# More modulation rows on TensorE, another order in the first layer, and padded pools, in a float32r network of two blocks

## The chip, the cores and the metric

One core of a Trainium2 chip runs the whole program. The metric is the device time of one execution in microseconds (us), the median of several. Before the change it is 2746.2 us (three runs, 2743.26 to 2751.51).

## The reference

The program computes two blocks on 512 tokens of width 1024, with 256 context tokens beside them in the first. The first block is two mixer layers with adaptive modulation by a condition vector; the change works mostly in the first of them:

```
m = silu(cond) @ w_mod + b_mod              # shift, scale, gate: 3 x 1024, for x and for the context
h = x * (1 + scale) + shift
z = h @ w_in                                # 1024 -> a, ga, u, v, gb of 512 each
ya = multiscale_pool(a) * silu(ga)          # windows 2, 4, 8, 16, then a 128x128 product per group
vn = (v - mean) * rsqrt(var + 1e-6)         # per token and head of 128
yb = u * (w_s @ vn + b_s) * silu(gb)        # per chunk of 128 tokens and head
x = layer_norm(alpha * x + gate * (concat(ya, yb) @ w_out))
```

The second layer is a Fourier mix beside a latent attention. The second block is twice: a gated feed-forward (1024 to 2816 to 1024), an attention of three kinds, and a second feed-forward.

## The kernel before

Activations lie with features on the 128 partitions and tokens along the free axis. Every product is kept near float32: each operand is split into a rounded float32r part H and the remainder L, and `mm3` issues three matmuls (H by H, H by L, L by H) into one PSUM bank. So the weights are split on the chip: `wload` fetches a 128x1024 block (tag `ws`, two buffers), ScalarE rounds it to `wh` (line 92), and `s.w_eng` subtracts for `wl` (line 93). `wnext` asks for blocks four ahead of the product that uses them, and each block fetched lets `s.rate` jobs of the list `s.jobs` go. The engine of line 93 is GpSimd (POOL) from the start of `ab`, the first layer, into the second; elsewhere it is mostly VectorE (DVE).

In `ab`, `mods(k)` makes two rows of modulation (k and 8 + k). A row in `ON_PE` is eight small float32 matmuls `pm` (line 548) and an addition on DVE (line 549); another is made on DVE by a custom multiply-and-reduce (line 475) for each of the two conditions, then line 552. These read `fbt`, silu of the condition on all partitions, which comes as a 1 MB transfer `crow` and passes ScalarE. `modx(k)` then modulates a block of tokens, and line 485 makes its L part on DVE. Six banks `pv` gather v, with the activations as stationary operand.

After that vn is normalised on DVE: statistics, an rsqrt of small operations (lines 194 to 202), and 24 operations at line 610. The projections `proj` stand in the order u, gb, u of the next head; after three of them come the six small matmuls `pf` (line 637), which need all of vn. DVE adds the bias, multiplies by u and by silu(gb), and splits the result into Y. The jobs in this time are the other modulation rows of this layer and all 24 of the next, two customs or one each, into borrowed buffers `xs` and `ctmp`. Then come the four pool groups (`pa`, `pb`, and `pp`, 128x128 products), and the output projection, which reads Y. A scheduler orders each engine's instructions.

Each tile pool begins where the pools opened before it end. `w` (weights) and `x` (activations and held blocks) begin 192 bytes past a multiple of 2048; the pools opened after the small pool `fc` begin elsewhere: `h` and `mo` (second block) and `fc` itself at 1856, `c`, `cdy`, `cdm`, `cda`, `cdf` at 384, `y` and `mw` and `yt` at 1632.

Of the kernel before, what the change touches and what calls it, by code (L numbers as in the profile page):

```python
# [9 lines left out]
F32 = mybir.dt.float32  # L10
F32R = mybir.dt.float32r
I32 = mybir.dt.int32
AF = mybir.ActivationFunctionType
ALU = mybir.AluOpType
# [3 lines left out]
P = 128  # L18
T = 512
NEG = -1e30  # L20
MAGIC = 0x5F3759DF
ALPHA = 4.0 ** 0.25
ON_PE = (0, 8, 10, 13, 15)
HALF = (slice(0, 256), slice(256, 512))
ALL = slice(0, 512)

# [5 lines left out]
class Net:  # L32
# [415 lines left out]
    def ab_weights(s):  # L448
        I = s.I
        for c in range(4):  # L450
            s.wpush(I["ab_v"][c], 1024)
        for i in (8, 12, 9, 13, 10, 14, 11, 15):
            s.wpush(I["ab_in"][i], 1024)
        s.wpush(I["pool_w"], 512)
        for i in (0, 4, 1, 5, 2, 6, 3, 7):
            s.wpush(I["ab_in"][i], 1024)
        for m in range(8):
            s.wpush(I["ab_out"][m], 1024)
# [55 lines left out]
    def ab(s):  # L514
        nc, tc, I = s.nc, s.tc, s.I
        s.psum(mm=range(6), t=(6, 7))
        s.w_eng = nc.gpsimd
        fbt = s.xp.tile([P, 4096], F32, tag="fb", name="fbt")
        s.first = ExitStack()
        s.fc = s.first.enter_context(tc.tile_pool(name="fc", bufs=1, reuse_waits="tile"))  # L520
# [2 lines left out]
        X = s.new_xh()  # L523
        C = [c_p.tile([P, 8, 256], F32R, tag="c" + t, name="c" + t) for t in "HL"]
        s.mods_start()
        b1 = c_p.tile([P, 16], F32, name="b1")
        nc.vector.tensor_copy(b1[:, 0:8], s.vec("ab_b", 0, 8))
        nc.vector.tensor_scalar(b1[:, 8:16], s.vec("ab_b", 8, 8), 1.0, None, op0=ALU.add)
        xs = s.xp.tile([P, 4096], F32, tag="x", name="xs")
        pv = [s.bank("pv") for _ in range(6)]  # L530

        def tokx(k, t):
            return s.xk(X, k, slice(t * P, t * P + P)) if t < 4 else s.xk(C, k, slice((t - 4) * P, (t - 3) * P))
# [6 lines left out]
        def mods(k):  # L540
            for m in (k, 8 + k):
                d = s.ab_m[:, m]
                if m in ON_PE:
                    w = mbuf()
                    nc.sync.dma_start(w, I["ab_mod"][m])
                    pm = s.bank("pm", "t")
                    for j in range(8):
                        nc.tensor.matmul(pm[:, 0:2], w[:, j * P:(j + 1) * P], s.sc[:, j], start=(j == 0), stop=(j == 7))
                    nc.vector.tensor_scalar(d, pm[:, 0:2], b1[:, m:m + 1], None, op0=ALU.add)
                else:  # L550
                    s.mod_dve(s.ab_m, I["ab_mod"], m, 2, fbt, mbuf)
                    nc.vector.tensor_scalar(d, d, b1[:, m:m + 1], None, op0=ALU.add)

        def modx(k):
            st = xs[:, k % 5 * 768:k % 5 * 768 + 768]
            nc.sync.dma_start(st, I["x"][:, k])
            s.modulate(X, k, ALL, st[:, :T], s.ab_m[:, 8 + k, 0:1], s.ab_m[:, k, 0:1], st[:, :T])
            s.modulate(C, k, slice(0, 256), st[:, T:], s.ab_m[:, 8 + k, 1:2], s.ab_m[:, k, 1:2], st[:, T:])
# [1 line left out]
        mods(0)  # L560

        for v in range(2):
            row = fbt[:, v * 1024:(v + 1) * 1024]
            nc.sync.dma_start(row, I["crow"][:, v * 1024:(v + 1) * 1024])
            nc.scalar.activation(row, row, AF.Silu)
        modx(0)
        mods(1)
        for k in range(8):
            if k % 2 == 0:
                W = s.wnext(1)  # L570
            if k < 7:
                modx(k + 1)
            if k < 6:
                mods(k + 2)
            w = [x[:, k % 2 * T:(k % 2 + 1) * T] for x in W]
            for t in range(6):
                s.mm3(pv[t], tokx(k, t), w, k == 0, k == 7)
        mx.close()
        ctmp = c_p.tile([P, 2048], F32, tag="cx", name="ctmp")
        spare = []  # L580

        def buf():
            spare.append(spare.pop(0))
            return spare[-1]
        spare += [xs[:, 3072:], ctmp[:, :1024], ctmp[:, 1024:]]
        nc.sync.dma_start(s.ident, I["ident"])
        nc.sync.dma_start(fbt[:, 2048:2560], I["sgu_b"])
        nc.sync.dma_start(fbt[:, 2560:3072], I["sgu_w"])
        edge = c_p.tile([P, 4, 16], F32, name="edge")
        nc.sync.dma_start(edge, I["edge"])  # L590
        with tc.tile_pool(name="y", bufs=1, reuse_waits="tile") as yp, tc.tile_pool(name="yt", bufs=1, reuse_waits="tile") as tp:
            Y = [yp.tile([P, 8, 768], F32R, name="y" + t) for t in "HL"]
# [11 lines left out]
            ve = c_p.tile([P, 24], F32, name="ve")  # L604
            nc.vector.tensor_scalar(ve, mv[:, :, 1], 1e-6, None, op0=ALU.add)
            rv = s.rsqrt(ve, 24, "sgu")
            for t in range(6):
                for h in range(4):
                    j = t * 4 + h
                    nc.vector.tensor_scalar(vn[:, t, h], vn[:, t, h], mv[:, j, 0:1], rv[:, j:j + 1], op0=ALU.subtract, op1=ALU.mult)  # L610

            def proj(ahead=4):

                W = s.wnext(ahead)
                a, b = s.bank("pa"), s.bank("pb")
                s.lin(a, W, X, 8, ALL)
                s.lin(b[:, :256], W, C, 8, slice(0, 256))
                return a, b[:, :256]
# [3 lines left out]
            def ysplit(k, src, sl):  # L622
                s.split(Y[0][:, k, sl], Y[1][:, k, sl], src)

            u = proj()
            for g in range(4):
                gb = proj()
                if g < 3:
                    u2 = proj()
                if g == 0:  # L630
                    s.jobs = [(lambda i=i: s.mod_dve(s.ab_m, I["ab_mod"], i, 2, fbt, buf)) for i in range(16, 24)]
                    s.jobs += [(lambda i=i: s.mod_dve(s.cd_m, I["cd_mod"], i, 2 if i < 16 else 1, fbt, buf)) for i in range(24)]
                G = tp.tile([P, 768], F32, tag="G", name="G")
                t_ = tp.tile([P, 768], F32, tag="T", name="T")
                pf = s.bank("pf", "t"), s.bank("pf", "t")
                for c in range(6):
                    nc.tensor.matmul(pf[c // 4][:, c % 4 * P:(c % 4 + 1) * P], vn[:, c, g], fbt[:, 2560 + g * P:2560 + (g + 1) * P], start=True, stop=True)
                for i, sl in enumerate(PARTS):
                    n = sl.stop - sl.start
                    bs = fbt[:, 2048 + g * P:2048 + (g + 1) * P].unsqueeze(1).to_broadcast([P, n // P, P])  # L640
                    tt = t_[:, sl]
                    nc.vector.tensor_tensor(tt.rearrange("p (c i) -> p c i", i=P), pf[i][:, :n].rearrange("p (c i) -> p c i", i=P), bs, op=ALU.add)
                    nc.scalar.activation(G[:, sl], gb[i], AF.Silu)
                    nc.vector.tensor_tensor(tt, tt, u[i], op=ALU.mult)
                    nc.vector.tensor_tensor(tt, tt, G[:, sl], op=ALU.mult)
                    ysplit(4 + g, tt, sl)
                u = u2


            LP = 800  # L650
            A, S1, S2 = ctmp[:, 0:LP], ctmp[:, LP:2 * LP], fbt[:, 3072:3072 + LP]
            spare[:] = [xs[:, j * 1024:(j + 1) * 1024] for j in range(4)]
            nc.gpsimd.memset(ctmp, 0.0)
            nc.gpsimd.memset(S2, 0.0)
            at = (slice(8, 520), slice(536, 792))
# [43 lines left out]
                old = new  # L699
            pool_out(3, *old)  # L700

            while s.jobs:
                s.jobs.pop(0)()
            s.add_bias(s.ab_m, "ab_b", 16, 24)

            nc.vector.tensor_scalar(s.ab_m[:, 16:24], s.ab_m[:, 16:24], 1.0 / ALPHA, None, op0=ALU.mult)
            s.add_bias(s.cd_m, "cd_b", 0, 16)
            s.add_bias(s.cd_m, "cd_b", 16, 24, 1)
            nc.vector.tensor_scalar(s.cd_m[:, 8:16], s.cd_m[:, 8:16], 1.0, None, op0=ALU.add)

            s.gb = s.fc.tile([P, 2, 8, 2], F32, name="gb")
            for v in range(2):
                nc.vector.tensor_tensor(s.gb[:, 0, :, v], s.cd_m[:, 8:16, v], s.vec("ab_g", 0, 8), op=ALU.mult)
                nc.vector.tensor_tensor(s.gb[:, 1, :, v], s.cd_m[:, 8:16, v], s.vec("ab_lb", 0, 8), op=ALU.mult)
                nc.vector.tensor_tensor(s.gb[:, 1, :, v], s.gb[:, 1, :, v], s.cd_m[:, 0:8, v], op=ALU.add)
            ag = c_p.tile([P, 2, 8], F32, name="ag")
            nc.vector.tensor_scalar(ag[:, 0], s.vec("ab_g", 0, 8), ALPHA, None, op0=ALU.mult)
            nc.vector.tensor_scalar(ag[:, 1], s.vec("ab_lb", 0, 8), ALPHA, None, op0=ALU.mult)
# [16 lines left out]
            def fin(m, seg, ps):  # L735
                v, sl = s.SEG[seg]
                s.ln_fin(V[v], m, sl, ps, s.ab_m[:, 16 + m, v:v + 1], acc[seg])

            for m in range(5):
                W = s.wnext()  # L740
                a, b = s.bank("pa"), s.bank("pb")[:, :256]
                omm(a, W, slice(0, T))
                omm(b, W, slice(T, 768))
                fin(m, 0, a[:, 0:256])
                fin(m, 1, a[:, 256:512])
                fin(m, 2, b)
            Ws = s.wlast(3)

            def last(seg, sl):
# [356 lines left out]
    def mix(s, l, st, mktail):  # L1106
# [12 lines left out]
        for k in range(8):  # L1119
            nc.sync.dma_start(s.spill[:, k], s.x[:, k])  # L1120

        ll = s.tp.tile([P, 2], F32, tag="ll", name="ll")
        nc.vector.tensor_tensor(ll, s.vec(f"lq_{l}", 0, 2), s.vec(f"lk_{l}", 0, 2), op=ALU.mult)
        pl = s.bank("pl", "t")
        nc.tensor.matmul(pl[:, 0:2], s.ones, ll, start=True, stop=True)
# [374 lines left out]
def prep_first(inp, A, vec):  # L1500
    i = lambda n: inp[n][0]
    cc = np.stack([i("c"), inp["c_ctx"]])
    vec("c", np.ascontiguousarray(cc.reshape(2, 8, P).transpose(2, 1, 0)).reshape(P, 16))
    A["crow"] = np.ascontiguousarray(np.broadcast_to(cc.reshape(1, 2048), (P, 2048)))
    vec("ab_b", rows(i("ab_b_mod")))
    vec("cd_b", rows(i("cd_b_mod")))
    vec("ab_g", rows(i("ab_ln_g")))
# [128 lines left out]
```

## Time and profile before

| | us |
|---|---|
| median of three runs | 2746.2 |
| lowest, highest | 2743.26, 2751.51 |
| profiled execution | 2743.77 |
| its span, first to last instruction | 2741.7 |
| PE busy in it | 2632.7 |
| DVE, ACT, POOL busy in it | 1504.3, 1056.6, 323.0 |

The profiled execution is 2.4 us below the median and 2.1 us above its own span. PE is TensorE, ACT ScalarE. PEclk is the clock granted to TensorE, as a share of its full level. A timeline row gives the start, the duration, and in brackets the idle time before and what ended it. A matmul's duration covers its passage through the array, so the pace of a run of matmuls is read from start to start; one row in float32 (line 548) counts two passes for each matmul of the code.

### The profile page before, as it was taken

How to read it: one execution, taken by the hardware profiler on the slowest of the kernel's cores; microseconds unless marked ns; L12 is line 12 of the kernel's file. 1: busy time of each engine (PE TensorE's matmuls, PEld its weight loads, DVE VectorE, ACT ScalarE, POOL GpSimd, SP SyncE). 2: the span in 40 equal slices, each digit the busy share in tenths (PEclk: the TensorE clock that was granted, in tenths of full speed). 3: DMA queues.
4: the chain of work that ended last, by engine and by line, in shares of the span. 5: the costliest groups of instructions: out<-in, count | busy, mean ns of one | idle time of the engine just before them, and what ended most of it. 6: DMA issues, size and time to landing. Idle time of an engine off the chain costs nothing. (4 is left out here: it accounts for less than half of the span.)

```text
span 2741.7 us, 36211 instructions
## 1 busy us (share of the span) xinstructions
PE 2632.7 (96%) x13676; PEld 2230.8 (81%) x13676; DVE 1504.3 (55%) x2886; ACT 1056.6 (39%) x1951; POOL 323.0 (12%) x300
## 2 busy tenths in 40 slices
PE   7898999998999999999999999999999998999998
PEld 6787987887888888878888888888888877988887
DVE  7895632888545345675853336633336666642434
ACT  4122533664444233454543224432223454432222
POOL 2323344003000011001200002000001001200000
PEclk9999999998999999999999999999999999999999
DMA  7353123004998247654693323963237655232221
GB/s 271 135 193 120 44 82 101 32 30 166 312 315 291 91 141 234 195 154 140 219 317 109 99 84 108 318 221 100 92 101 243 208 156 156 76 100 99 94 94 60
DMA packets 133966, 418.15 MB, mean 153 GB/s; under 512 B 17376, under 2 KB 20960, under 8 KB 133792
## 3 DMA queue, kind: packets, MB, share of 16 engines
q1 hardware_dynamic: 133792, 415.84, 45.7%
q8 instruction: 108, 1.77, 0.3%
q14 instruction: 66, 0.54, 0.1%
HBM read 314.32 MB, written 73.40 MB: 141 GB/s over the span
## 5 line engine op out<-in xcount | busy, mean ns | idle before, releaser
L92 ACT ACTIVATE wh<-ws 128x1024 fp32r<-128x1024 f32 (+2 forms) x335 | 345.3, 1033 | 865.4 <-PE pd L148 238.6
L93 DVE TENSOR_TENSOR wl<-ws,wh 128x1024 fp32r<-128x1024 f32 (+1 forms) x267 | 318.3, 1192 | 164.4 <-ACT wh L92 161.1
L147 PE MATMUL pg<-xH,wh 128*128 128x512 f32 x672 | 262.2, 390 | 0.0
L149 PE MATMUL pg<-xH,wl 128*128 128x512 f32 x672 | 261.7, 389 | 0.0
L148 PE MATMUL pg<-xL,wh 128*128 128x512 f32 x672 | 261.6, 389 | 0.0
L149 PE MATMUL pd<-hH,wl 128*128 128x512 f32 x632 | 249.6, 395 | 0.0
L147 PE MATMUL pd<-hH,wh 128*128 128x512 f32 x632 | 249.6, 395 | 0.0
L148 PE MATMUL pd<-hL,wh 128*128 128x512 f32 x632 | 249.6, 395 | 0.0
L148 PE MATMUL pu<-xL,wh 128*128 128x512 f32 x640 | 249.2, 389 | 0.0
L147 PE MATMUL pu<-xH,wh 128*128 128x512 f32 x640 | 249.1, 389 | 0.0
L149 PE MATMUL pu<-xH,wl 128*128 128x512 f32 x640 | 249.0, 389 | 0.0
L93 POOL TENSOR_TENSOR wl<-ws,wh 128x1024 fp32r<-128x1024 f32 (+1 forms) x68 | 171.5, 2529 | 326.1 <-ACT wh L92 317.0
L247 POOL TENSOR_TENSOR accf<-accf,sq 128x256 f32<-128x256 f32 x48 | 39.7, 847 | 1390.1 <-ACT sq L246 1390.1
L399 DVE TENSOR_TENSOR ht<-ht,pu 128x512 f32<-128x512 f32 x80 | 54.9, 686 | 182.5 <-PE pu L149 180.4
L149 PEld LDWEIGHTS pg<-xH,wl 128*128 128x128 f32 x672 | 126.1, 188 | 26.1
L148 PEld LDWEIGHTS pg<-xL,wh 128*128 128x128 f32 x672 | 126.2, 188 | 26.0
L147 PEld LDWEIGHTS pg<-xH,wh 128*128 128x128 f32 x672 | 126.2, 188 | 26.1
L148 PEld LDWEIGHTS pd<-hL,wh 128*128 128x128 f32 x632 | 118.6, 188 | 28.8
L149 PEld LDWEIGHTS pd<-hH,wl 128*128 128x128 f32 x632 | 118.6, 188 | 28.8
L147 PEld LDWEIGHTS pd<-hH,wh 128*128 128x128 f32 x632 | 118.6, 188 | 28.7
L147 PEld LDWEIGHTS pu<-xH,wh 128*128 128x128 f32 x640 | 120.1, 188 | 25.0
L148 PEld LDWEIGHTS pu<-xL,wh 128*128 128x128 f32 x640 | 120.1, 188 | 24.9
(622 smaller groups left out, 5982.6 us busy)
## 6 DMA issues: line engine op xcount, KB each, us to landing
ws<-ffn_gate SPq DMA_DIRECT2D x88, 512.0 KB, 3.5
ws<-ffn_up SPq DMA_DIRECT2D x88, 512.0 KB, 3.5
hl<-eh SPq DMA_DIRECT2D x64, 512.0 KB, 6.8
hl<-el SPq DMA_DIRECT2D x64, 512.0 KB, 6.8
ws<-ffn_down SPq DMA_DIRECT2D x64, 512.0 KB, 3.6
wh<-hl SPq DMA_DIRECT2D x58, 512.0 KB, 4.3
wl<-hl SPq DMA_DIRECT2D x58, 512.0 KB, 6.0
es<-wqk SPq DMA_DIRECT2D x32, 512.0 KB, 5.8
```

Of the source, the lines that this page charges most:

```text
L92: nc.scalar.activation(wh[:, :n], st[:, :n], AF.Copy)
L93: s.w_eng.tensor_tensor(wl[:, :n], st[:, :n], f(wh[:, :n]), op=ALU.subtract)
L147: mm(out, A[0], B[0], start=start, stop=False)
L148: mm(out, A[0], B[1], start=False, stop=False)
L149: mm(out, A[1], B[0], start=False, stop=stop)
L247: (eng or nc.gpsimd).tensor_tensor(acc[0], acc[0], sq, op=ALU.add)
L399: nc.vector.tensor_tensor(t, t, pu, op=ALU.mult)
```

## The change

The first layer: three more rows of modulation go to PE (1, 9, 12 and 14 for 13), so the rows of both first blocks are made there. `crow` goes: sixteen float32 matmuls `pr` (line 566) spread silu(c) over the partitions, and ScalarE copies them to `fbt`. Line 93 is on DVE in `ab` as elsewhere. Half of vn's normalisation goes to ScalarE (with nb = -mean * rstd), head by head. Jobs get three buffers of their own, `mj`, and wait for the last DVE instruction of the normalisation; they go at 1.4 per block instead of 2.2. The head loop starts with two u projections, and does `pf`, the bias and the product with u ahead of the gb projection. The rest of the jobs and what reads the second layer's rows move behind five output projections.

The padding: `b1` moves to `fc`, and `gb`, `edge` and `ll` get a longer tile, so that `fc` is 2048 bytes. It begins at 131264 instead of 130880, which is 192 past a multiple of 2048, and so do after it `h`, `mo`, `ma`, `c`, `cdy`, `cdm`, `cda`, `cdf`, `y` and `yt`.

```diff
-ON_PE = (0, 8, 10, 13, 15)
+ON_PE = (0, 1, 8, 9, 10, 12, 14, 15)
-        s.w_eng = nc.gpsimd
+        s.w_eng = nc.vector
+        nc.sync.dma_start(s.ident, I["ident"])
-        b1 = c_p.tile([P, 16], F32, name="b1")
+        b1 = s.fc.tile([P, 16], F32, name="b1")
...
         for v in range(2):
-            row = fbt[:, v * 1024:(v + 1) * 1024]
-            nc.sync.dma_start(row, I["crow"][:, v * 1024:(v + 1) * 1024])
-            nc.scalar.activation(row, row, AF.Silu)
+            for h in range(2):
+                pr = s.bank("pr")
+                for j in range(4):
+                    nc.tensor.matmul(pr[:, j * P:(j + 1) * P], s.sc[:, 4 * h + j, v:v + 1].to_broadcast([P, P]), s.ident, start=True, stop=True)
+                nc.scalar.activation(fbt[:, v * 1024 + h * T:v * 1024 + (h + 1) * T], pr, AF.Copy)
...
+        buf = lambda: c_p.tile([P, 1024], F32, tag="mj", name="mj", bufs=3)
-        edge = c_p.tile([P, 4, 16], F32, name="edge")
+        edge = c_p.tile([P, 256], F32, name="edge")[:, :64].rearrange("p (g t) -> p g t", t=16)
...
-            for t in range(6):
-                for h in range(4):
+            nb = c_p.tile([P, 24], F32, name="nb")
+            nc.vector.scalar_tensor_tensor(nb, mv[:, :, 0], -1.0, rv, op0=ALU.mult, op1=ALU.mult)
+            for h in range(4):
+                for t in range(6):
                     j = t * 4 + h
-                    nc.vector.tensor_scalar(vn[:, t, h], vn[:, t, h], mv[:, j, 0:1], rv[:, j:j + 1], op0=ALU.subtract, op1=ALU.mult)
+                    if t % 2:
+                        nc.scalar.activation(vn[:, t, h], vn[:, t, h], AF.Identity, scale=rv[:, j:j + 1], bias=nb[:, j:j + 1])
+                    else:
+                        normed = nc.vector.tensor_scalar(vn[:, t, h], vn[:, t, h], mv[:, j, 0:1], rv[:, j:j + 1], op0=ALU.subtract, op1=ALU.mult)
...
-            u = proj()
+            us = [proj(), proj()]
+            s.rate = 1.4
             for g in range(4):
-                gb = proj()
-                if g < 3:
-                    u2 = proj()
...
+                    nc.vector.tensor_tensor(tt, tt, us[g][i], op=ALU.mult)
+                gb = proj()
+                if g < 2:
+                    us.append(proj())
...
-            while s.jobs:
+            while len(s.jobs) > 24:
                 s.jobs.pop(0)()
...
+            s.gb = s.fc.tile([P, 384], F32, name="gb")[:, :32].rearrange("p (a m v) -> p a m v", a=2, m=8)
...
-        ll = s.tp.tile([P, 2], F32, tag="ll", name="ll")
+        ll = s.tp.tile([P, 56], F32, tag="ll", name="ll")[:, :2]
```

PE at the start of the program; `pm` is a row of modulation, `pr` the spread condition, `pv` the v projection. Before:

```order
L548 MATMUL pm_175<-sc_156,wm_173 128x2 x8
L548 MATMUL pm_187<-sc_156,wm_185 128x2 x8
L147 MATMUL pv_164<-wh_224,xH_152 128x512
L147 MATMUL pv_165<-wh_224,xH_152 128x512
L148 MATMUL pv_164<-wl_225,xH_152 128x512
L149 MATMUL pv_164<-wh_224,xL_153 128x512
L148 MATMUL pv_165<-wl_225,xH_152 128x512
L149 MATMUL pv_165<-wh_224,xL_153 128x512
```

After:

```order
L566 MATMUL pr_192<-ident_76,sc_156 128x128
L548 MATMUL pm_170<-sc_156,wm_168 128x2 x8
L566 MATMUL pr_192<-ident_76,sc_156 128x128 x3
L548 MATMUL pm_182<-sc_156,wm_180 128x2 x8
L566 MATMUL pr_198<-ident_76,sc_156 128x128 x4
L566 MATMUL pr_204<-ident_76,sc_156 128x128 x4
L566 MATMUL pr_210<-ident_76,sc_156 128x128 x4
L548 MATMUL pm_231<-sc_156,wm_229 128x2 x8
L147 MATMUL pv_253<-wh_225,xH_152 128x512
L147 MATMUL pv_254<-wh_225,xH_152 128x512
L548 MATMUL pm_243<-sc_156,wm_241 128x2 x8
L147 MATMUL pv_255<-wh_225,xH_152 128x512
```

Two rows of modulation stood ahead of the first `pv`; now it is three and the sixteen `pr`, and a fourth row stands after two more matmuls.

DVE at the end of vn's rsqrt; `junk` names the customs of the jobs, `tsgu` and `ysgu` are the rsqrt's, `xs` is vn. Before:

```order
L198 SCALAR_TENSOR_TENSOR tsgu<-tsgu 128x24
L475 ISA junk,ab_m<-ctmp,fbt 128x1024
L475 ISA ab_m 128x1
L199 SCALAR_TENSOR_TENSOR ysgu<-tsgu,ysgu 128x24
L475 ISA junk,ab_m<-xs,fbt 128x1024
L475 ISA ab_m 128x1
L200 TENSOR_TENSOR tsgu<-ysgu 128x24
L475 ISA junk,ab_m<-xs,fbt 128x1024
L475 ISA ab_m 128x1
L201 SCALAR_TENSOR_TENSOR tsgu<-tsgu,ve 128x24
L202 SCALAR_TENSOR_TENSOR ysgu<-tsgu,ysgu 128x24
L610 TENSOR_SCALAR xs<-xs,mv,ysgu 128x128 x24
```

After, from the same place to the end of the normalisation:

```order
L93 TENSOR_TENSOR wl<-ws,wh 128x1024
L194 TENSOR_SCALAR ysgu<-ve 128x24
L196 TENSOR_TENSOR tsgu<-ysgu 128x24
L197 TENSOR_TENSOR tsgu<-tsgu,ve 128x24
L198 SCALAR_TENSOR_TENSOR tsgu<-tsgu 128x24
L199 SCALAR_TENSOR_TENSOR ysgu<-tsgu,ysgu 128x24
L200 TENSOR_TENSOR tsgu<-ysgu 128x24
L201 SCALAR_TENSOR_TENSOR tsgu<-tsgu,ve 128x24
L202 SCALAR_TENSOR_TENSOR ysgu<-tsgu,ysgu 128x24
L606 SCALAR_TENSOR_TENSOR nb<-mv,ysgu 128x24
L613 TENSOR_SCALAR xs<-xs,mv,ysgu 128x128 x12
L475 ISA junk,ab_m<-mj,fbt 128x1024
```

The customs have gone from between the rsqrt's operations, one of line 93 stands ahead of them (another one earlier), and DVE normalises 12 blocks instead of 24.

## Rows read from the trace of the kernel before

**Rows 1.** The page, engines: busy time, share of the span, instructions.
```profile
PE 2632.7 (96%) x13676; PEld 2230.8 (81%) x13676; DVE 1504.3 (55%) x2886; ACT 1056.6 (39%) x1951; POOL 323.0 (12%) x300
```

**Rows 2.** The first layer by windows: length, busy of five engines, PEclk, DMA share, GB/s.
```profile
80.00:100.00 20.00, 15.96 (x73) 12.88 (x72) 19.86 (x42) 3.37 (x5) 9.05 (x3) 0.79 0.42 145
100.00:120.00 20.00, 16.55 (x81) 13.69 (x81) 19.17 (x34) 2.44 (x5) 2.89 (x2) 0.87 0.40 136
200.00:220.00 20.00, 16.89 (x84) 14.26 (x84) 19.93 (x38) 4.08 (x8) 5.66 (x2) 0.91 0.52 179
220.00:240.00 20.00, 11.12 (x57) 9.12 (x56) 15.83 (x22) 7.63 (x16) 5.48 (x2) 0.79 0.56 175
```

**Rows 3.** PE's waits, first 330 us: total us, times, longest.
```profile
PE pp L147 <- ACT yH L236: 11.1, 2, 8.9
...
PE pf L637 <- DVE xs L610: 4.0, 6, 2.7
...
PE pa L147 <- DVE T L644: 3.4, 1, 3.4
```

**Rows 4.** DVE's timeline, 33 to 97 us: start, duration, operation.
```profile
33.05 3.30 DVE L475 CUSTOM_DVE_ANT_0 junk<-wm,fbt 128x1024 bf16<-128x1024 f32 x1
...
36.53 1.22 DVE L475 CUSTOM_DVE_ANT_0 junk<-wm,fbt 128x1024 bf16<-128x1024 f32 x1
...
57.75 0.22 DVE L552 TENSOR_SCALAR ab_m<-ab_m,b 128x2 f32<-128x2 f32 x1
...
66.88 1.68 DVE L603 BATCH_NORM_AGGREGATE mv<-bns 128x2 f32<-128x6 f32 x24
...
73.48 2.37 DVE L196 TENSOR_TENSOR tsgu<-ysgu 128x24 f32<-128x24 f32 x1
...
88.92 8.42 DVE L610 TENSOR_SCALAR xs<-xs,mv,ysgu 128x128 f32<-128x128 f32 x24
```

**Rows 5.** PE's timeline at the start of the kernel.
```profile
5.50 6.96 PE L548 MATMUL pm<-sc,wm 128*128 128x2 f32 x32 [5.50 <-DMA wm<-ab_mod]
16.25 1.22 PE L147 MATMUL pv<-wh,xH 128*128 128x512 f32 x2 [3.79 <-ACT wh L92]
...
23.99 1.84 PE L548 MATMUL pm<-sc,wm 128*128 128x2 f32 x16
```

**Rows 6.** The page, line 93 on its two engines: busy, mean ns, idle before.
```profile
L93 DVE TENSOR_TENSOR wl<-ws,wh 128x1024 fp32r<-128x1024 f32 (+1 forms) x267 | 318.3, 1192 | 164.4 <-ACT wh L92 161.1
...
L93 POOL TENSOR_TENSOR wl<-ws,wh 128x1024 fp32r<-128x1024 f32 (+1 forms) x68 | 171.5, 2529 | 326.1 <-ACT wh L92 317.0
```

**Rows 7.** Windows 64 to 247 and 480 to 620 us, all engines.
```profile
64.00:247.00 183.00, 162.25 (x891) 140.18 (x890) 157.45 (x287) 43.13 (x73) 59.70 (x22) 0.93 0.48 167
...
480.00:620.00 140.00, 136.16 (x865) 115.82 (x864) 116.71 (x251) 92.40 (x242) 10.39 (x8) 1.00 0.09 31
```

**Rows 8.** The same first window, DVE at line 475 alone.
```profile
64.00:247.00 183.00, 83.56 (x112) 0.93 0.48 167
```

**Rows 9.** Windows of PE in five unbroken runs of matmuls.
```profile
753.09:797.88 44.79, 44.79 (x193) 1.00 0.89 304
797.88:884.94 87.06, 87.06 (x386) 1.00 0.90 312
246.71:252.10 5.39, 5.39 (x26) 1.00 0.22 66
277.64:290.10 12.46, 12.46 (x107) 1.00 0.21 78
1318.69:1337.24 18.55, 18.55 (x158) 1.00 0.48 165
```

**Rows 10.** PE's timeline, three score matmuls of the second layer.
```profile
515.88 0.39 PE L147 MATMUL pS<-r 128*128 128x512 f32 x1
516.12 0.40 PE L148 MATMUL pS<-r 128*128 128x512 f32 x1
516.35 0.39 PE L149 MATMUL pS<-r 128*128 128x512 f32 x1
```

More of the change, by code (lines that the diff above doesn't have):

```diff
@@ L451, in ab_weights @@
             s.wpush(I["ab_v"][c], 1024)
-        for i in (8, 12, 9, 13, 10, 14, 11, 15):
+        for i in (8, 9, 12, 10, 13, 11, 14, 15):
             s.wpush(I["ab_in"][i], 1024)
@@ L529, in ab @@
         xs = s.xp.tile([P, 4096], F32, tag="x", name="xs")
-        pv = [s.bank("pv") for _ in range(6)]
         def tokx(k, t):
@@ L562, in ab @@
         for v in range(2):
-            row = fbt[:, v * 1024:(v + 1) * 1024]
-            nc.sync.dma_start(row, I["crow"][:, v * 1024:(v + 1) * 1024])
-            nc.scalar.activation(row, row, AF.Silu)
+            for h in range(2):
[3 more added lines that the diff above has]
+                nc.scalar.activation(fbt[:, v * 1024 + h * T:v * 1024 + (h + 1) * T], pr, AF.Copy)
         modx(0)
+        s.wload(1)
         mods(1)
+        pv = [s.bank("pv") for _ in range(6)]
         for k in range(8):
@@ L579, in ab @@
         ctmp = c_p.tile([P, 2048], F32, tag="cx", name="ctmp")
[L580 to L586, printed above, removed]
+        buf = lambda: c_p.tile([P, 1024], F32, tag="mj", name="mj", bufs=3)
         nc.sync.dma_start(fbt[:, 2048:2560], I["sgu_b"])
         nc.sync.dma_start(fbt[:, 2560:3072], I["sgu_w"])
-        edge = c_p.tile([P, 4, 16], F32, name="edge")
+        edge = c_p.tile([P, 256], F32, name="edge")[:, :64].rearrange("p (g t) -> p g t", t=16)
         nc.sync.dma_start(edge, I["edge"])
@@ L623, in ysplit, with after_v, run @@
                 s.split(Y[0][:, k, sl], Y[1][:, k, sl], src)
-            u = proj()
-            for g in range(4):
-                gb = proj()
-                if g < 3:
-                    u2 = proj()
[L630 to L634, printed above, removed]
+            def after_v(*a):
+                def run():
+                    with tc.issue_after(normed.ins):
+                        s.mod_dve(*a, fbt, buf)
+                return run
+            us = [proj(), proj()]
+            s.jobs = [after_v(s.ab_m, I["ab_mod"], i, 2) for i in range(16, 24)]
+            s.jobs += [after_v(s.cd_m, I["cd_mod"], i, 2 if i < 16 else 1) for i in range(24)]
+            s.rate = 1.4
+            for g in range(4):
                 pf = s.bank("pf", "t"), s.bank("pf", "t")
@@ L637, in ab @@
                     nc.tensor.matmul(pf[c // 4][:, c % 4 * P:(c % 4 + 1) * P], vn[:, c, g], fbt[:, 2560 + g * P:2560 + (g + 1) * P], start=True, stop=True)
+                t_ = tp.tile([P, 768], F32, tag="T", name="T")
                 for i, sl in enumerate(PARTS):
@@ L642, in ab @@
                     nc.vector.tensor_tensor(tt.rearrange("p (c i) -> p c i", i=P), pf[i][:, :n].rearrange("p (c i) -> p c i", i=P), bs, op=ALU.add)
+                    nc.vector.tensor_tensor(tt, tt, us[g][i], op=ALU.mult)
+                gb = proj()
+                if g < 2:
+                    us.append(proj())
+                G = tp.tile([P, 768], F32, tag="G", name="G")
+                for i, sl in enumerate(PARTS):
                     nc.scalar.activation(G[:, sl], gb[i], AF.Silu)
[L644 to L647, printed above, removed]
+                    nc.vector.tensor_tensor(t_[:, sl], t_[:, sl], G[:, sl], op=ALU.mult)
+                    ysplit(4 + g, t_[:, sl], sl)
             LP = 800
             A, S1, S2 = ctmp[:, 0:LP], ctmp[:, LP:2 * LP], fbt[:, 3072:3072 + LP]
-            spare[:] = [xs[:, j * 1024:(j + 1) * 1024] for j in range(4)]
             nc.gpsimd.memset(ctmp, 0.0)
@@ L706, in ab @@
             nc.vector.tensor_scalar(s.ab_m[:, 16:24], s.ab_m[:, 16:24], 1.0 / ALPHA, None, op0=ALU.mult)
[L707 to L715, printed above, removed]
             ag = c_p.tile([P, 2, 8], F32, name="ag")
@@ L746, in ab @@
                 fin(m, 2, b)
+            while s.jobs:
+                s.jobs.pop(0)()
+            s.add_bias(s.cd_m, "cd_b", 0, 16)
+            s.add_bias(s.cd_m, "cd_b", 16, 24, 1)
+            nc.vector.tensor_scalar(s.cd_m[:, 8:16], s.cd_m[:, 8:16], 1.0, None, op0=ALU.add)
+            s.gb = s.fc.tile([P, 384], F32, name="gb")[:, :32].rearrange("p (a m v) -> p a m v", a=2, m=8)
+            for v in range(2):
+                nc.vector.tensor_tensor(s.gb[:, 0, :, v], s.cd_m[:, 8:16, v], s.vec("ab_g", 0, 8), op=ALU.mult)
+                nc.vector.tensor_tensor(s.gb[:, 1, :, v], s.cd_m[:, 8:16, v], s.vec("ab_lb", 0, 8), op=ALU.mult)
+                nc.vector.tensor_tensor(s.gb[:, 1, :, v], s.gb[:, 1, :, v], s.cd_m[:, 0:8, v], op=ALU.add)
             Ws = s.wlast(3)
@@ L1503, in prep_first @@
     vec("c", np.ascontiguousarray(cc.reshape(2, 8, P).transpose(2, 1, 0)).reshape(P, 16))
-    A["crow"] = np.ascontiguousarray(np.broadcast_to(cc.reshape(1, 2048), (P, 2048)))
     vec("ab_b", rows(i("ab_b_mod")))
```

## The prediction

> **What bounds the kernel now.** I read the engines' shares first. PE is busy for 2632.7 of 2741.7 us [rows 1]: the kernel is bound by PE, and there are two ways to make it faster: fill PE's gaps, or make its matmuls follow each other at a shorter pace. Then I cut the first layer into windows, because most of the diff lies there. The windows from 80 to 120 and from 200 to 240 us [rows 2] are those in which PE stands idle for longest, and PEclk falls in them too, to 0.79 at the worst. In the same windows DVE is nearly always busy except in the last. PE's waits name what it waits for [rows 3]: vn from line 610 (`pf`), then the product T of line 644, and at the end of the layer `yH`, which comes out of DVE's line behind the jobs. So DVE limits this layer. Last I took long unbroken runs of matmuls, where nothing waits, and divided the window by the number of starts in it [rows 9] (the counts in the rows include neighbours that reach in: the runs have 192, 384, 23, 105 and 154). These show the pace of each pair of operands.
>
> **The start.** The condition's 16 `pr` and a third row `pm` come ahead of the first `pv`. Before, 32 passes of `pm` took 6.96 us at the start, 0.22 each, and 16 passes 1.84 us, 0.115 each, later [rows 5]. The 16 `pr` are float32, so 32 passes; taken like the early passes they cost 7.0 us, and the third row 3.5. From 5.5 that is 3 x 3.5 + 7.0 = 17.5, so the first `pv` would start at 23 instead of 16.25 [rows 5], nearly 7 later. Against that stands the side of DVE: it finished the last modulation row at 57.75 [rows 4], and it loses three rows (six customs of 1.22, [rows 4]) and gets about four of line 93 at 1.19 [rows 6], 2.5 us less, and no custom is stretched any more (below). If the passes go at the later pace, `pr` and `pm` take 7.4 and nothing is lost; the 1 MB of `crow` gone may even let rows land sooner. Bounds -1.4 and +5.7; I take +4.5, near the cold row, because PE's first 20 us in the trace all have that pace.
>
> **The wait for vn.** In 80 to 120 PE is idle for 4.04 + 3.45 us, and the lower clock takes (0.21 + 0.13) x 20 = 6.8 [rows 2]: 14.3 lost. The chain behind it: statistics end at 68.5, the normalisation begins only at 88.92 and takes 8.42 [rows 4]. Between them stand customs of the jobs, eight of them, and rsqrt operations of up to 2.37 us on 128x24 elements [rows 4]. After, DVE's order has no job there, no POOL work beside it, and 12 blocks instead of 24: some 2 us for the small operations, two of line 93 (2.4) and 4.2 for the 12 blocks, while ScalarE does the others. With the 4.6 that statistics took after the last `pv`, vn is there about 13 us after it, and two projections (48 matmuls, 8.3 us each by [rows 9]) cover 16.6. I take all 14.3. A bound on the other side is 9, if the half on ScalarE goes as slowly as DVE's 24 did, since ScalarE also rounds the weights there.
>
> **The end of the layer.** In 200 to 240 idle time is 3.11 + 8.88, and the clock's part (0.09 + 0.21) x 20 = 6.0: 18.0 lost [rows 2]. It is DVE's backlog, so I add up DVE. From 64 to 247 it is busy for 157.5 of 183 [rows 7], of which line 475 has 83.56 in 56 customs and their reads [rows 8], 1.49 a custom. A custom beside POOL's line 93 took 3.30, one alone 1.22 [rows 4]; with its read the undisturbed one needs 1.27. Line 93 leaves POOL, so 56 x 0.22 = 12.4 goes. The rsqrt gives 4 x 2.2 = 8.8, the normalisation 4.2, stretched additions perhaps 8. About 20 of line 93 come, at 1.19 [rows 6]: +23.8. DVE then needs about 148 in a stretch of some 161. It fits, but not by much, so I leave 4 of the 18 and take -14. Bounds -18 and -4.
>
> **New waits.** The six banks of PSUM are now held by two u and a gb ahead of time. The second and third heads' projections want a bank that is free only after DVE has multiplied by u. That is the wait of `pa` for T, 3.4 us once in before [rows 3]. I take it twice, less the part that a shorter line on DVE saves: +6, bounds 0 and +10.
>
> **Behind the layer.** 29 of line 93 move to DVE in the second layer. Where DVE has most to do, in 480 to 620, it is busy for 116.7 of 140, and POOL has eight instructions there [rows 7]; at 1.19 they cost DVE under 10 and find 23. The layer's closing normalisation loses its competition with POOL. I take -1.5, bounds -3 and +3. The second layer's rows are asked for by the same jobs as before, whose order on DVE stays ahead of the output projections, so moving the last of them behind five projections is worth nothing; `ll`, `edge`, `gb` and `b1` cost nothing in themselves, since they only lengthen tiles.
>
> **The padding.** 192 matmuls of 512 columns that stream `hH` or `hL` take 44.79 us, 233.3 ns each; 384 that stream `xH` or `xL` against the same weights take 87.06, 226.7 each [rows 9]. DMA was at 0.89 and 0.90 in these two, so it is not the DMA. In the pools before, x and w begin at the same place modulo 2048, h does not. The four feed-forwards have 1896 such matmuls, counted in the program: 1896 x 6.6 = 12.5 us. Some 750 others of 512 columns have an operand in `mo`, `ma`, `y`, `c` or `cd*`; the run of `y` gives 5.39 / 23 = 234 [rows 9]; at 6.5 they add 4.9. At 256 columns the sign turns: 105 with `y` took 118.7 each, 154 with x 120.5 [rows 9]; 1500 matmuls of 256 columns at 1.5 give 2.2 back. Sum -15.2. Bounds: -17 and, if only the short ones change, +2.
> The Trainium skill speaks against this term: SBUF — State Buffer, in "Who interferes with whom", says that PE and ACT never wait on anyone, and TensorE: Matmul & The Clock Gate, in "Step-by-step: what each phase is for", that streamed operand and weights have read ports of their own. By that an address could not matter and the term would be 0. The two rows with the same weights and the same clock differ by 6.6 ns for some reason, so the trace does not settle it for the rule; I hold that as the first rival.
>
> **The sum.** 2743.8 + 4.5 - 14.3 - 14 + 6 - 1.5 - 15.2 = 2709.3 us. The profiled execution is 2.4 below the median of its runs, so the median should be 2711.7; I say 2712.
>
> **Rivals.**
> 1. The address does nothing, and h is slower for another reason. For it: every slow operand lies behind the first 130,880 bytes, so place and alignment can't be told apart, and three score matmuls with both operands in x, aligned, also follow at 0.24 and 0.23 us [rows 10]. Against it: weights are read from the same place in both runs of [rows 9], and the 256-column sign would be strange for a far address. Then 2712 + 15 = 2727.
> 2. The start does not cost anything and the new waits stay hidden: with TensorE busy sooner, the early passes run at the pace of the 16 [rows 5]. Then 2712 - 4.5 - 6 = 2701, or a few less.
> 3. The layer gets half of what I give it: DVE has 148 of 161 only if all of my savings come. If vn gains 9, the end 4 and the waits cost 10, it yields 1.5 less 4.5 at the start, so with the padding about 2734, and without it 2749.
> 4. Slower: DVE is the bound of the layer and line 93 makes it worse. If the customs' 1.49 [rows 8] is not POOL's doing, DVE needs 157.5 + 23.8 - 4.2 = 177 where 161 were wanted. It decides from a need over 161: 16 of the gain of 28 go; two thirds of the eight in 480 to 620 land on a chain that PE waits for (+6), the start costs 5.7, and with a padding that does nothing or +2 the time is 2743.8 + 5.7 - 14.3 - 14 + 16 + 6 + 6 + 2 + 2.4 = 2754. Against it: the pairs 3.30 and 1.22 of one instruction [rows 4] stand beside POOL's activity and away from it.
>
> **Chances.** The forecast 0.60, the first rival 0.14, the second 0.13, the third 0.09, the fourth 0.04. A measurement of this kernel tells about 0.3% from no change, 8 us. Faster by more: 0.60 + 0.14 + 0.13 and half of the third, 0.91; within: 0.05; slower: 0.04. The likeliest case alone spans 2702 to 2722 by the bounds of its terms, since not all go one way. The range reaches down to the second rival with the larger bounds of the end (-18) and the padding (-17), and a little below, 2693, and up past the first to most of the third, 2733.
>
> **What would show it.** In the profile after: the feed-forward's down projections at 226.7 ns from start to start (233 means the first rival); no wait of `pf` for vn and PEclk 1.00 from 80 to 120 us; `pf` first at about 85 us instead of 89 to 105; line 475 at 1.22 throughout; the first `pv` at about 23 us and the last at about 69 (63.9 before); the wait of `pp` for `yH` at 3 or 4 us; and DVE below 95% from 64 us to the output projection. I am wrong if DVE stays full there and PE's waits on it stay at 15 us or more, or if line 93 in the second layer shows up among the releasers of PE.

## The result and the profile after

The changed kernel takes 2699.93 us (median of four runs, 2697.05 to 2703.04) against 2746.72 of the kernel before beside it: a ratio of 0.9829, interval 0.9809 to 0.9848, so 47 us faster. 2712 with 2693 to 2733 was predicted.

First the page's engines and line 93, which answer to [rows 1, 6]; no row of POOL is left for it among the large groups.

```profile
PE 2614.4 (97%) x13756; PEld 2234.4 (83%) x13756; DVE 1506.0 (56%) x2923; ACT 1062.3 (39%) x1965; POOL 172.0 (6%) x240
...
L93 DVE TENSOR_TENSOR wl<-ws,wh 128x1024 fp32r<-128x1024 f32 (+2 forms) x327 | 390.0, 1194 | 229.6 <-ACT wh L92 223.8
```

POOL has lost 151 us of work and DVE has gained only 1.7, though it does 60 more instructions of line 93 (72 us): its other instructions became shorter, and some moved to PE and ScalarE. PE is busy for 18 us less with 80 instructions more, which is pace and clock.

The windows of [rows 2], in the same columns (PE, PEld, DVE, ACT, POOL, PEclk):

```profile
80.00:100.00 20.00, 20.00 (x122) 17.86 (x121) 18.83 (x31) 7.79 (x12) 0.00 (x0) 1.00 0.60 196
100.00:120.00 20.00, 18.92 (x115) 16.61 (x115) 19.79 (x36) 3.61 (x6) 0.00 (x0) 1.00 0.68 212
200.00:220.00 20.00, 20.00 (x119) 17.47 (x117) 12.64 (x21) 6.89 (x12) 0.00 (x0) 1.00 0.26 83
220.00:240.00 20.00, 20.00 (x113) 17.43 (x113) 9.61 (x15) 4.24 (x7) 4.34 (x6) 1.00 0.32 109
```

PE is full and at PEclk 1.00 in all four, but for 1.08 us. Of its waits in the first 330 us, as [rows 3], the longest that does not belong to the start is this:

```profile
...
PE pa L147 <- DVE T L649: 1.1, 1, 1.1
```

Neither `pf` for vn nor `pp` for `yH`, of which 3 or 4 us were expected to stay, is in the list. The start, as [rows 5]:

```profile
5.66 3.58 PE L548 MATMUL pm<-sc,wm 128*128 128x2 f32 x16 [1.72 <-DMA wm<-ab_mod]
...
13.79 4.67 PE L566 MATMUL pr<-ident,sc 128*128 128x128 f32 x24
18.29 1.84 PE L548 MATMUL pm<-sc,wm 128*128 128x2 f32 x16
20.57 0.99 PE L147 MATMUL pv<-wh,xH 128*128 128x512 f32 x2 [0.44 <-ACT wh L92]
21.36 3.41 PE L548 MATMUL pm<-sc,wm 128*128 128x2 f32 x16
```

The last 24 passes of `pr` take 4.67, 0.19 each, and the third `pm` row 1.84, the later pace of [rows 5], but the fourth row 3.41 again. PE alone under the third row and under the fourth:

```profile
17.60:20.80 3.20, 2.76 (x25) 1.00 0.57 228
21.00:27.60 6.60, 6.60 (x25) 0.50 0.72 220
```

The clock is full under the third and at the lower of its two levels (1.2 of 2.4 GHz) under the fourth; before it fell, PE had worked for 2.76 of 3.20 us, with one wait of 0.44 for `wh`. The first two rows go at the slow pace as well, 3.58 and 3.41, though the profile gives PEclk 1.00 there; no row shows why. The first `pv` starts at 20.57 instead of 16.25, and the first projection at 67.3 instead of 63.9. DVE after the last `pv`, as [rows 4], and the first `pf` on PE:

```profile
70.05 1.68 DVE L601 BATCH_NORM_AGGREGATE mv<-bns 128x2 f32<-128x6 f32 x24
71.64 1.20 DVE L93 TENSOR_TENSOR wl<-ws,wh 128x1024 fp32r<-128x1024 f32 x1
...
74.18 0.18 DVE L196 TENSOR_TENSOR tsgu<-ysgu 128x24 f32<-128x24 f32 x1
...
75.80 3.16 DVE L613 TENSOR_SCALAR xs<-xs,mv,ysgu 128x128 f32<-128x128 f32 x12
78.89 1.21 DVE L475 CUSTOM_DVE_ANT_0 junk<-mj,fbt 128x1024 bf16<-128x1024 f32 x1
```

```profile
83.94 1.50 PE L642 MATMUL pf<-fbt,xs 128*128 128x128 f32 x12
```

The rsqrt's 2.37 are 0.18, and DVE's half of vn is there at 79, five before PE asks; `pf` waits for nothing. From 64 to 222 us (the output projection begins at 210.8), all engines and then line 475 alone, as [rows 7, 8]:

```profile
64.00:222.00 158.00, 156.92 (x910) 138.07 (x909) 143.29 (x302) 50.51 (x87) 0.00 (x0) 1.00 0.58 191
```

```profile
64.00:222.00 158.00, 68.80 (x112) 1.00 0.58 191
```

68.80 for 56 customs with their reads is 1.23 each; it was 1.49 [rows 8]. DVE is busy for 143.3 of 158. Last, runs of matmuls as in [rows 9]: h, x, y at 512 columns and y at 256:

```profile
720.67:764.19 43.52, 43.52 (x193) 1.00 0.91 313
764.19:851.23 87.04, 87.04 (x385) 1.00 0.91 312
229.00:234.25 5.25, 5.25 (x26) 1.00 0.23 73
251.15:263.74 12.59, 12.59 (x106) 1.00 0.13 45
```

44.79 has become 43.52, 226.7 ns each, and x is as it was. y went from 234 to 5.25 / 23 = 228 at 512 columns, a run of only 23, and from 118.7 to 12.59 / 105 = 119.9 at 256.

### The profile page after: what moved, and what is told of

Read it like the earlier page. It is cut to its first block, busy times and chain, and to the rows that moved or that the text cites. A ratio compares the mean times of both kernels' runs of the same rounds, so it can differ in the third digit from the quotient of the medians.

```text
span 2695.3 us, 36338 instructions
## 1 busy us (share of the span) xinstructions
PE 2614.4 (97%) x13756; PEld 2234.4 (83%) x13756; DVE 1506.0 (56%) x2923; ACT 1062.3 (39%) x1965; POOL 172.0 (6%) x240
## 5 line engine op out<-in xcount | busy, mean ns | idle before, releaser
L92 ACT ACTIVATE wh<-ws 128x1024 fp32r<-128x1024 f32 (+2 forms) x335 | 345.3, 1033 | 839.7 <-PE pd L148 226.6
L93 DVE TENSOR_TENSOR wl<-ws,wh 128x1024 fp32r<-128x1024 f32 (+2 forms) x327 | 390.0, 1194 | 229.6 <-ACT wh L92 223.8
L149 PEld LDWEIGHTS pu<-xH,wl 128*128 128x128 f32 x640 | 120.2, 188 | 25.1
L237 DVE TENSOR_TENSOR el<-es,eh 128x1024 fp32r<-128x1024 f32 x64 | 78.2, 1222 | 106.7 <-DMA hl<-el 81.2
```

Source lines behind the costliest of these rows:

```text
L92: nc.scalar.activation(wh[:, :n], st[:, :n], AF.Copy)
L93: s.w_eng.tensor_tensor(wl[:, :n], st[:, :n], f(wh[:, :n]), op=ALU.subtract)
L149: mm(out, A[1], B[0], start=False, stop=stop)
L237: s.nc.vector.tensor_tensor(L, src, f(H), op=ALU.subtract)
```

## The experiments

The first stage ends at the first projection, each other one at the first matmul of what its column names: the first output projection, the sums of the closing norm, the Fourier product of the second layer (`spec`), the halves that end that layer (`pdh`), and the last matmul. Each is from one profiled execution, in us.

| run | line 93 | order | padding | start | to output | to norm | to Fourier | to halves | to end | median |
|---|---|---|---|---|---|---|---|---|---|---|
| before | POOL | old | no | 63.9 | 160.9 | 65.4 | 92.3 | 227.0 | 2123.0 | 2743.5 to 2746.7 |
| e1_pad_only | POOL | old | yes | 63.5 | 162.3 | 63.9 | 92.1 | 226.1 | 2107.1 | 2729.7 |
| e3_split_on_pool | POOL | new | yes | 74.3 | 166.1 | 55.5 | 90.3 | 226.3 | 2108.9 | 2732.5 |
| e6_split_on_dve | DVE | old | no | 63.5 | 141.7 | 53.3 | 88.5 | 227.5 | 2123.7 | 2709.0 |
| e2_layer_only | DVE | new | no | 69.5 | 142.2 | 53.1 | 85.1 | 227.6 | 2121.4 | 2711.6 |
| e8_split_and_pad | DVE | old | yes | 63.4 | 143.2 | 53.1 | 87.3 | 226.5 | 2107.4 | 2692.4 |
| after | DVE | new | yes | 67.3 | 143.5 | 53.1 | 86.7 | 226.6 | 2108.8 | 2697.4 to 2699.9 |

"New order" stands for all the edits in the first layer but line 93 and the padding: rows on PE, `pr`, the normalisation, the jobs, the head loop.

**The padding alone**, e1_pad_only: the kernel before with longer tiles (here `edge` has 280 columns, which puts y at the same place).

```diff
...
-            s.gb = s.fc.tile([P, 2, 8, 2], F32, name="gb")
+            s.gb = s.fc.tile([P, 384], F32, name="gb")[:, :32].rearrange("p (a m v) -> p a m v", a=2, m=8)
...
-        ll = s.tp.tile([P, 2], F32, tag="ll", name="ll")
+        ll = s.tp.tile([P, 56], F32, tag="ll", name="ll")[:, :2]
```

> The kernel before with nothing but the paddings (b1, gb, edge and ll longer tiles, so that every pool of streamed operands begins 192 bytes past a multiple of 2048, as the weights do). Theory (the place of the operands modulo 512 bytes sets the pace): 512-column matmuls with h go from 233.3 to 226.7 ns, 256-column ones from 118.7 to about 120, the whole becomes 13 to 17 us faster than before and the first layer keeps its gaps at 80 to 120 and 200 to 240 us. Rival (the gain of 47 us is all the first layer's order): within 3 us of before, h at 233 ns.

2729.68 against 2745.12, ratio 0.9944 (0.9928 to 0.9960): 15.4 us. The run of h that was 44.79:

```profile
753.00:796.51 43.51, 43.51 (x193) 1.00 0.90 308
```

**The first layer alone**, e2_layer_only: the changed kernel with the lines above taken back.

> The changed kernel without the paddings: pools of streamed operands begin where they did before (h at 1856 modulo 2048). Theory: h back at 233.3 ns, the rest of the gain stays, so 13 to 17 us slower than the changed kernel, 30 to 33 faster than before; with e1 the two gains add up to 47. Rival (the two parts need each other, for example because the first layer's gain comes from y and c at another place): the sum of the two gains differs from 47 by more than 6.

2711.61 against 2745.12, ratio 0.9884 (0.9867 to 0.9901): 33.5 us. With e1 that makes 48.9, and both together make 47: the two add up. The same run of h in it:

```profile
720.13:764.92 44.79, 44.79 (x194) 1.00 0.90 308
```

**The place by itself**, e5_offsets. Its loop, with W the weights and M the streamed tile:

```python
for i in range(count):
    a = o + (i % 8) * 512
    b = (i % 16) * 128
    nc.tensor.matmul(ps[:, :n], W[:, b:b + 128], M[:, a:a + n], start=i == 0, stop=i == count - 1)
```

> The disputed cost by itself: none of the reference is computed, only runs of 48 matmuls, streamed operand against changing weights, all zeros in float32r, with the streamed tile at 0, 16, 32, 64, 128, 192, 256, 320, 384, 448, 512 and 1024 bytes from the weights' place modulo 512 or 2048, at 512 and at 256 columns, and at 0 and 128 bytes in a tile that lies beyond 117,000 bytes. Theory (place modulo 512 decides): at 512 columns 226.7 ns at 0, 512 and 1024 bytes and 232 to 235 at 64 to 448, near and far alike; at 256 columns 120 at 0 and 117.5 to 119 elsewhere. Rival (modulo 2048 decides): 512 and 1024 bytes are as slow as 128. Rival (the place in memory decides): far is 233 at 0 and at 128, near 226.7 at both.

The last 32 starts of nine of its runs (each run has 48; the first starts come less evenly): at 512 columns 0, 128, 256 and 1024 bytes, then 0 and 128 in the far tile; at 256 columns 0, 128 and 192 bytes.

```profile
55.97:63.22 7.25, 7.25 (x34) 1.00 0.43 181
101.57:109.03 7.46, 7.46 (x33) 1.00 0.00 0
124.55:131.80 7.25, 7.25 (x34) 1.00 0.00 0
181.37:188.63 7.26, 7.26 (x34) 1.00 0.00 0
192.65:199.90 7.25, 7.25 (x34) 1.00 0.00 0
203.93:211.40 7.47, 7.47 (x34) 1.00 0.00 0
213.88:217.72 3.84, 3.84 (x35) 1.00 0.00 0
237.86:241.66 3.80, 3.80 (x35) 1.00 0.00 0
243.82:247.44 3.62, 3.62 (x34) 1.00 0.00 0
```

Divided by 32: 226.7 at 0, 256 and 1024 bytes, 233 at 128, near and far alike; at 256 columns 120.0, 118.7 and 113.3. The rivals of place in memory and of modulo 2048 both fall, and my modulo 512 too: 256 bytes are as good as 0. **A shift by 256**, e7_shift_256, tries that in the whole kernel:

```diff
-        ll = s.tp.tile([P, 56], F32, tag="ll", name="ll")[:, :2]
+        ll = s.tp.tile([P, 88], F32, tag="ll", name="ll")[:, :2]
```

> The changed kernel with every pool of streamed operands 256 bytes further on, so at 448 modulo 2048 against 192 for the weights. Theory (the place modulo 256 bytes sets the pace, as in the isolated runs, where 256 bytes gave 226.7 ns and 128 gave 233): h at 226.7 ns, the whole within 3 us of the changed kernel. Rival (the place modulo 2048 must be that of the weights): h at 229 to 235 ns, 5 to 16 us slower.

2698.80, beside 2697.79 for the changed kernel on that chip; h at 43.52 again:

```profile
722.43:765.95 43.52, 43.52 (x193) 1.00 0.90 306
```

So the streamed operand and the weights need to agree modulo 256 bytes, and not more. Both runs moved the streamed operand against weights that stayed; whether it is the two together that count, or the streamed operand's own place, they don't separate.

**Line 93 back on POOL**, e3_split_on_pool:

```diff
-        s.w_eng = nc.vector
+        s.w_eng = nc.gpsimd
```

> The changed kernel with line 93 on POOL again in the first layer and in the second up to its tail. Theory (POOL's line 93 beside DVE is what stretched DVE's instructions): customs of 3.3 us and rsqrt operations of 2.4 us come back, the closing layer norm of the first layer and the second layer's start are late again by 6 to 9 us, in all 10 to 20 us slower than the changed kernel. Rival (the order in the head loop and the normalisation without jobs in it did it): within 4 us of the changed kernel, since DVE then has about 24 us less to do from 64 to 222 us.

2732.47, ratio 0.9954 (0.9938 to 0.9970) to before: some 33 us slower than the changed kernel, more than either theory said, 7 of it in the start. PE's waits and two of DVE's customs in it:

```profile
PE pa L147 <- DVE T L649: 11.0, 3, 6.1
PE pf L642 <- DVE T L648: 4.2, 1, 4.2
```

```profile
89.83 3.33 DVE L475 CUSTOM_DVE_ANT_0 junk<-mj,fbt 128x1024 bf16<-128x1024 f32 x1
...
93.20 3.30 DVE L475 CUSTOM_DVE_ANT_0 junk<-mj,fbt 128x1024 bf16<-128x1024 f32 x1
```

The long customs are back, and with them waits for T and for `pf`'s bank: 15.2 us, where the changed kernel has 1.1. This is the new wait of the prediction; it is long only when DVE is late.

**Line 93 moved, nothing else**, e6_split_on_dve: the kernel before with that one line the other way.

> The kernel before with one line changed: line 93 on DVE in the first layer and the second, nothing else, no padding and no other order. Theory (POOL's line 93 is what slows DVE, and moving it is most of the first layer's gain): 15 to 28 us faster than before, customs at 1.22, the wait for vn at line 610 shorter by 9 to 12 us. Rival (it is the order and the move together, since DVE's line with the jobs in it gets 35 us more work): within 6 us of before, or slower.

2708.98 against 2743.93, ratio 0.9867 (0.9852 to 0.9882): 35 us, all that the first layer gains and more, and beyond what either theory allowed. The windows of [rows 2] in it (in 220 to 240 PE is busy for 20.00, at PEclk 1.00), and DVE:

```profile
80.00:100.00 20.00, 19.81 (x118) 17.27 (x117) 19.86 (x50) 3.93 (x6) 0.00 (x0) 1.00 0.44 139
100.00:120.00 20.00, 20.00 (x119) 17.57 (x118) 18.76 (x34) 4.26 (x7) 0.97 (x1) 1.00 0.52 181
200.00:220.00 20.00, 20.00 (x113) 17.03 (x112) 15.44 (x35) 7.67 (x14) 0.00 (x0) 1.00 0.72 240
```

```profile
71.83 0.17 DVE L196 TENSOR_TENSOR tsgu<-ysgu 128x24 f32<-128x24 f32 x1
71.95 1.22 DVE L475 CUSTOM_DVE_ANT_0 junk<-xs,fbt 128x1024 bf16<-128x1024 f32 x1
...
81.48 6.24 DVE L610 TENSOR_SCALAR xs<-xs,mv,ysgu 128x128 f32<-128x128 f32 x24
```

The jobs still stand between the rsqrt's operations, and DVE still normalises 24 blocks, but each piece has its short duration, the 24 blocks begin at 81.48 instead of 88.92, and PE hardly waits. The move has a second effect that could be the cause: DVE makes `wl` in 1.19 us where POOL took 2.53 [rows 6], so the weights are ready sooner. But PE waited for `wl` once in the first 330 us, before and in e6 alike:

```profile
PE pv L148 <- POOL wl L93: 1.7, 1, 1.7
```

```profile
PE pv L148 <- DVE wl L93: 1.7, 1, 1.7
```

**The transfer instead of `pr`**, e4_crow_dma and, beside the changed kernel on one chip, e4_again and after_again.

```diff
-            for h in range(2):
-                pr = s.bank("pr")
...
+            row = fbt[:, v * 1024:(v + 1) * 1024]
+            nc.sync.dma_start(row, I["crow"][:, v * 1024:(v + 1) * 1024])
+            nc.scalar.activation(row, row, AF.Silu)
```

> The changed kernel with the 1 MB transfer of the condition and its silu on ScalarE instead of the sixteen float32 matmuls pr and four copies. Theory (the pr passes cost the start): the first pv starts 4 to 6 us sooner than at 20.6, and the last pv ends 3 us sooner than at 67.3, so 2 to 4 us faster than the changed kernel. Rival (the start is set by the rows of modulation that arrive and DVE's work on them): no change within 1.5 us, or slower by up to 4 because 1 MB more comes in the first 20 us, where DMA is at 0.87.

> The variant with the 1 MB transfer instead of pr once more, beside the changed kernel on one chip. Theory (what it gains in the first layer is given back in that layer's closing norm, where both reach the second layer's scores at 437.7 and 437.9 us in their traces): within 2 us of the changed kernel. Rival (its first median, 3.7 us lower, is real): 3 to 5 us faster than the changed kernel.

> The changed kernel once more, on the chip of the two runs beside it. All theories: within 4 us of its first median of 2699.9.

2696.20 the first time; then 2695.09 (2692.63 to 2696.75) beside 2697.79 (2697.24 to 2698.94). The first `pv` starts at 17.1 and 17.6 and the first projection at 65.8 and 66.1, against 67.3 and 68.8. The second layer's Fourier product begins at 350.7 and 350.6, against 350.5 and 350.1: the 1.5 to 2.7 are given back in the closing norm. Its first part and then the whole of it, from its sums to the Fourier product, in e4_again and after that in after_again, in the columns above:

```profile
260.00:280.00 20.00, 19.78 (x150) 19.42 (x149) 13.34 (x43) 8.66 (x21) 2.23 (x3) 0.91 0.01 4
261.95:350.57 88.62, 85.86 (x589) 79.54 (x588) 60.14 (x161) 51.99 (x99) 17.64 (x22) 0.96 0.17 60
```

```profile
260.00:280.00 20.00, 19.78 (x161) 19.33 (x161) 12.64 (x40) 7.03 (x17) 1.49 (x2) 1.00 0.01 4
264.97:350.07 85.10, 82.78 (x590) 76.50 (x588) 59.95 (x161) 51.56 (x99) 17.91 (x22) 1.00 0.18 62
```

PE's clock falls there in the one and not in the other, and (1 - 0.96) x 88.62 = 3.5 is the whole difference. PE was busy for 19.78 of the first 20 us in both, so these rows don't show what made it fall. Between the medians lie 2.7 us and the intervals of the ratios overlap (0.9807 to 0.9836, 0.9815 to 0.9848): whether it is faster as a whole stays open.

**Two parts without the rest**, e8_split_and_pad (e1 with e6's line), beside after_third:

> The kernel before with two of the change's parts alone: line 93 on DVE, and the paddings; the order of the first layer, the condition's transfer, the jobs and the normalisation are those of before. Theory (line 93 is worth 35 us, the padding 15, and the rest of the first layer's edits costs 2 to 3): about 2694 us, 2 to 6 us faster than the changed kernel beside it. Rival (with the padding, too, the new order is worth something): as fast as the changed kernel or slower.

> The changed kernel beside the run of two parts, on one chip: within 3 us of 2697.8, its last median.

2692.41 (2690.72 to 2694.99) and 2697.43 (2696.16 to 2699.63): e8 is the faster, by 5 us, and the fastest kernel of the study. Its first `pv`:

```profile
15.75 1.65 PE L147 MATMUL pv<-wh,xH 128*128 128x512 f32 x3 [3.79 <-ACT wh L92]
```

The table places the difference: the start, 63.4 against 67.3 (68.8 and 69.1 in the two repeats of the changed kernel). From the first to the output projection both take 143.

## Why the prediction was right, and where it was not

The forecast was 34 us faster and 47 came; direction and range held. By its own steps, with the table's stages:

- **The start**, +4.5: +3.3, and 4.9 and 5.1 in the repeats. Right, but the rows do not all run at one pace: the first, second and fourth took 3.4 to 3.6, the third, at full clock, 1.84.
- **The wait for vn**, -14.3: gone, as forecast, but not for the reason that filled most of the paragraph. e6 shows that jobs between the rsqrt's operations and 24 blocks on one engine do no harm once POOL is quiet; e3 has the new order and a slow DVE, and PE waits elsewhere in its place.
- **The end of the layer**, -14: the wait went wholly. DVE needed 143.3 in 158 where 148 in 161 was reckoned, and I left 4 us for a line that is this full; they weren't needed.
- **New waits**, +6: 1.1. This is the term that was most mis-sized. I priced it by a wait of before [rows 3], whose length was itself DVE's delay, after having removed that delay in the step ahead.
- **Behind the layer**, -1.5: -5.6 to the Fourier product and -0.4 to the halves. I had gone by DVE's load there and not by PE's clock. From the closing norm's sums to the Fourier product, before and after, PEclk in the third column from the end:

```profile
290.23:382.52 92.29, 88.23 (x590) 81.50 (x588) 55.21 (x151) 51.94 (x99) 40.72 (x33) 0.93 0.17 57
```

```profile
263.86:350.55 86.69, 84.33 (x590) 78.08 (x588) 60.05 (x161) 51.57 (x99) 17.92 (x22) 0.98 0.18 61
```

  (1 - PEclk) is worth 0.07 x 92.3 = 6.5 us before and 0.02 x 86.7 = 1.7 after. Without it 85.8 and 85.0 are left, and 85.1 in e4_again and after_again: nearly all of this gain is the clock's. Before, PE also waited 1.9 us for a DVE rsqrt beside POOL's line 93; that wait is gone after, but the stage is hardly shorter for it. Why the clock fell, no run shows.
- **The padding**, -15.2: -15.4 in e1; from e2's 33.5 to the changed kernel's 46.0 to 46.8 it is -12.5 to -13.3. Right, the turned sign at 256 columns too.

By stages the miss of 12 us is this: from the first projection to the closing norm 226.3 became 196.6, 29.7 less where 14.3 + 14 - 6 = 22.3 was forecast; behind it 6.0 instead of 1.5; the start 1.2 better; the padding some 1 less. The first comes from costs that a late DVE makes, which went with the lateness: e6, whose only edit is line 93, has 195.0 there. The second is nearly all the clock's, which moves from run to run: the stage that was 86.7 here took 85.1 and 85.0 in the repeats of the changed kernel, and 88.5 in e6. That it has to do with DVE's lateness is not shown.

Of the rivals, the first (the address does nothing) fell with e1 and e5. The rule that spoke for it, in the Trainium skill, SBUF — State Buffer, "Who interferes with whom" (PE never waits on another engine), does not cover this: the same matmul took 226.7 or 233.3 ns in e5 by the place of one operand, while DVE and POOL were busy for 0.00 in those windows. The second rival's number, 2701, was the closest, through one of its two halves: the waits stayed hidden, the start did cost. The third fell too: the layer gave more than the forecast, not half. The fourth fell with e6: there 56 customs with their reads take 68.71 us from 64 to 205, 1.23 each, so 1.49 was POOL's doing. That agrees with the same section of the Trainium skill, by which a DVE instruction with two SBUF inputs contends with a GpSimd one that reads SBUF; 3.30 against 1.22 is its price here.

Two sums of the prediction are off, without touching the forecast. Three rows and `pr` are 80 passes, so 9.2 us at the later pace and not 7.4; and in the third rival 9 + 4 - 10 makes 3 and not 1.5, which puts it at 2732.5.

What was wrong is the credit. I shared the first layer's gain out among its edits, and the study gives all of it to one line: with line 93 on POOL the rest of the edits is worth +2.8 us (e1 to e3), with it on DVE +2.6 without padding (e6 to e2) and +5.0 with it (e8 to after). The 2.6 and 2.8 are differences of medians a few us wide, and e2 and e6 ran on two chips (against the kernel before on each, 33.5 and 35.0 us); they say little more than that there is no gain.

## What to carry to other kernels

When an engine that shares memory with another is late, price the sharing first: compare the same instruction beside the neighbour's work and away from it, and ask what the late engine's whole line would be at the short durations, before reordering anything. A wait taken from the trace as the price of a new wait must be taken after the steps that shorten it. Long unbroken runs of one instruction, divided by their count, show differences of 3% in pace that no list of waits can show.

## What the runs showed of the hardware

A float32r matmul of 512 columns follows the one before by 226.7 ns when streamed operand and weights lie alike modulo 256 bytes and by 229 to 233 at the eight other places tried in e5; near and far tile gave the same. The weights were never moved, so the streamed operand's own place may be all that counts. At 256 columns it is the other way: 120.0 alike, 113.3 at 192 bytes. Why, no run here shows; nor why c at 192 bytes, in the kernel before, took 117.7 (69.40 to 72.11 us, 23 matmuls) and not 113.3.

A DVE instruction of 0.18 us on 24 columns took up to 2.37 beside one of POOL's, about as long as that one lasts (2.53, [rows 6]). In the kernel before, two of line 93 on POOL, and the DVE instruction that stood beside the second:

```profile
72.53 6.72 POOL L93 TENSOR_TENSOR wl<-ws,wh 128x1024 fp32r<-128x1024 f32 x2 [2.59 <-ACT wh L92]
```

```profile
76.92 2.36 DVE L197 TENSOR_TENSOR tsgu<-tsgu,ve 128x24 f32<-128x24 f32 x1
```

POOL ends at 79.25 and DVE at 79.28: the small instruction lasted until POOL was done. The 24 blocks of the normalisation, 8.42 us with one of line 93 beside them, took 6.24 in e6. So 60 instructions of POOL, off the path, cost the path 35 us, by e6.
